# Moving the attention's keys and values beside two projections, and scoring the context in one product

## The chip, the cores and the metric

The kernel runs on one core of a Trainium2 chip. The metric is device time in microseconds (us) of one execution. Before the change the median of three runs was 2660.58 us (2660.32 to 2667.91).

A core has a matrix engine (PE; its weight loads are shown as a row of their own, PEld), a vector engine (DVE), a scalar engine (ACT), a general engine (POOL) and a queue engine for transfers (SP). Each runs its own list of instructions in order and waits on semaphores for the others. Products land in PSUM; DVE and ACT read them from there.

## The reference, cut to what matters

The reference is a transformer block with two mixers, an attention and a gated delta rule, followed by a second block. Only the first block's attention and its neighbours matter here:

```python
aq, ak, av, dq, dk, dv, ... = split_cols(h @ w_in)        # 512 latent tokens
..., cak, cav, ...          = split_cols(hc @ w_in)       # 256 context tokens
q_a  = axial_rope(rms_norm(heads(aq, 8), q_norm_g), row, col)
k_a  = axial_rope(rms_norm(heads(ak, 2), k_norm_g), row, col)
k_ac = rms_norm(heads(cak, 2), k_norm_g)
# per block of 128 queries and per head: at most three blocks of latent keys
# (a band of +-128), all 256 context keys and a sink logit in one softmax
s_loc = where(valid, q @ k_band * 0.125, -1e30);  s_ctx = q @ k_ctx * 0.125
p = softmax(concat([s_loc, s_ctx, s_sink]));      o = p[loc] @ v_band + p[ctx] @ v_ctx
```

There are 8 query heads in two groups that share a key and a value head each, head size 64, and four query blocks: 4 x 2 units of 4 heads, 32 pairs of a head and a query block in all.

## The kernel before, in words

Every large product is made three times with operands split into a rounded and a remainder part (`whi`, `wlo`; `hh`, `hl`), all in the helper `mm3_steps` (L447), which yields after each 8 matmuls. Weights come in blocks of 1 MB through SP's queue (`fetch_w`), are split by ACT (L435) and by DVE or POOL (L108), and two blocks of split weights are held.

In `block1` the projections run one after another. `dense_fm` makes channels on partitions; the short convolution `conv` reads its products out of PSUM on ACT and DVE (L621 to L626), turns them into tokens one tile later (L632) and writes them to DRAM. `dense_tm` makes tokens on partitions; the attention's queries are copied to `aq` by ACT (L658). The order is: keys of the delta rule, its values ("v", two blocks, `dense_fm`), the attention's queries (two blocks, `dense_tm`), and then `rest`: "q" of the convolution and three gates, 72 steps of 8 matmuls.

The attention runs beside the first 28 steps of `rest`. `weave` (through `side_by_side`) takes steps of several generators in turn, in proportion to the numbers that stand beside them:

```python
kv, units = self.window_attention(c, akv, aq, yA)
self.weave((self.take(rest, 28), 28), (self.seq(kv, units), 130))
```

`kv` (19 steps) makes the rotation tables, and for each of six tiles of 128 tokens the norm (`head_rms`: ACT square, DVE sum, POOL power), the rotation (DVE and POOL, L1204 to L1211), the split keys `ks` (ACT L1263, DVE L1264), the split values, and three steps later four transposes (`turn`, L1279) whose result DVE copies into `kT` (L1281). `units` (111 steps) then runs `prep(0)` (the queries of one block: norm, rotation, split `qs`, transposes L1305, copy to `QT` L1307), `front` of the first unit and, for each unit, `back` beside the `front` of the next and the `prep` of the next query block. `front` makes the scores of four heads: two products with the band's keys (L1322, L1323), masks (L1326), four products of 128 columns with the context's keys (L1329), then the row maximum on DVE (L1331), the exponential on ACT (L1335) and, after four heads, the division (L1344). `back` transposes the weights (L1360), splits them (L1363, L1364) and multiplies by the values (L1354).

All of the attention's memory is opened when it starts (`wa1`, `wa2`, and `psS` in PSUM), after the pool of the convolution has been closed. All other PSUM products go through `psum`, which gives four buffers in turn. The context manager is opened with `schedule_with_timeline_sim=True`: the order of the instructions on each engine is laid out when the program is built, from estimated times, and need not be that of the code; on the chip it is fixed.

After the attention the delta rule's first part (`delta`, L904 to L969) runs beside the other 44 steps of `rest`.

Of the kernel before, what the change touches and what calls it, by code (L numbers as in the profile page):

```python
# [78 lines left out]
class Trunk:  # L79
# [438 lines left out]
    def block1(self):  # L518
        nc, I, v = self.nc, self.I, self.v
        b1 = ExitStack()  # L520
# [79 lines left out]
        x_st = [(2 + t, (h[0], h[1], t * P)) for t in range(4)]  # L600
# [6 lines left out]
        evc = ExitStack()  # L607
        kvs = ExitStack()
        evk = self.pool("ev0", 4, side="right", ctx=kvs)
        dgs = ExitStack()  # L610
# [69 lines left out]
        dgs.close()  # L680
        self.dense_fm(0, 2, [cm, xm], conv("v", 8, evk))
        self.dense_tm(0, 2, x_st, keep_aq)

# [15 lines left out]
        with ExitStack() as c:  # L699
            kv, units = self.window_attention(c, akv, aq, yA)  # L700
            self.weave((self.take(rest, 28), 28), (self.seq(kv, units), 130))
            self.flush()
        evc.close()

        yAs = ExitStack()
# [507 lines left out]

    def window_attention(self, ctx, akv, aq, yA):

        nc, I = self.nc, self.I
        one = self.pool("wa1", 1, side="right", ctx=ctx)
        two = self.pool("wa2", 2, side="right", ctx=ctx)
        psc = self.pool("psS", 2, PSUM, ctx=ctx)
        mR = self.T(one, (P, 2, P), "mR", F32R)  # L1220
# [13 lines left out]

        def kv():
            nc.scalar.activation(mR, self.cst[:, C_WP:C_WP + 2 * P].rearrange("p (a b) -> p a b", b=P), AF.Copy)
# [9 lines left out]
            for tt in range(6):  # L1246
                key = tt - 2 if tt >= 2 else tt + 4
                k = akv[:, tt, 0:128].rearrange("p (h f) -> p h f", f=64)
                r = self.head_rms(one, k, 2, "k")
                yield  # L1250
                kn = self.T(one, (P, 2, 64), "kn")
                nc.vector.tensor_tensor(kn, k, r.unsqueeze(2).to_broadcast([P, 2, 64]), ALU.mult)
                if tt >= 2:
                    C, Sn = tabs["k"]
                    kr = self.T(two, (P, 2, 64), "kr")
# [27 lines left out]

        def prep(n):

# [22 lines left out]

        def front(u):
            n, g = u["n"], u["g"]  # L1310
            b0, b1 = max(n - 1, 0), min(n + 1, 3)
            nl = b1 - b0 + 1
            W = nl * P + 256
            u["kb"] = kb = [(b0 + i, i * P) for i in range(nl)] + [(4, nl * P), (5, nl * P + P)]
            Pt = u["Pt"] = self.T(two, (P, 4, 640), "Pt")
            mx = self.T(two, (P, 4), "mx")
            ssum = self.T(two, (P, 4), "ssum")
            for j in range(4):
                h = 4 * g + j
                ps = self.T(psc, (P, 1024), "sc")  # L1320
                lq = QT[n][:, h, :]
                nc.tensor.matmul(ps[:, :nl * P], lq, kT[:, g, 0, b0 * P:(b1 + 1) * P], start=True, stop=False)  # L1322
                nc.tensor.matmul(ps[:, :nl * P], lq, kT[:, g, 1, b0 * P:(b1 + 1) * P], start=False, stop=False)  # L1323
                edge = ([(0, 0)] if n > 0 else []) + ([(1, (nl - 1) * P)] if n < 3 else [])
                for i, (m, o) in enumerate(edge):
                    nc.tensor.matmul(ps[:, o:o + P], self.identR, mR[:, m, :], start=False, stop=i == len(edge) - 1)  # L1326
                for cx, o in kb[nl:]:
                    for w in range(2):
                        nc.tensor.matmul(ps[:, o:o + P], lq, kT[:, g, w, cx * P:(cx + 1) * P],  # L1329
                                         start=w == 0, stop=w == 1)  # L1330
                nc.vector.tensor_reduce(mx[:, j:j + 1], ps[:, :W], AX.X, ALU.max)  # L1331

                nc.vector.tensor_scalar(mx[:, j:j + 1], mx[:, j:j + 1], -0.125, nsink[:, h:h + 1],
                                        ALU.mult, ALU.min)
                nc.scalar.activation(Pt[:, j, :W], ps[:, :W], AF.Exp, bias=mx[:, j:j + 1], scale=0.125,  # L1335
                                     accum_out=ssum[:, j:j + 1])
                yield
# [8 lines left out]

        def back(u):
            n, g, kb, Pt = u["n"], u["g"], u["kb"], u["Pt"]
# [28 lines left out]

        def units():
            us = [dict(n=n, g=g) for n in range(4) for g in range(2)]
            yield from prep(0)  # L1380
            yield from front(us[0])
            for i, u in enumerate(us):
                nxt = us[i + 1] if i + 1 < len(us) else None
                n = u["n"] + 1
                yield from self.side_by_side(
                    (back(u), 11), (front(nxt) if nxt else None, 5), (prep(n) if u["g"] == 0 and n < 4 else None, 6))

        return kv(), units()


# [615 lines left out]
```

## Time and profile before

| | |
|---|---|
| median of three runs | 2660.58 us |
| the profiled execution | 2655.62 us, its span 2653.8 us |
| busy share: PE, DVE, ACT, POOL | 93%, 56%, 38%, 33% |
| mean granted clock of PE | 0.958 of full speed |

The span is what the profiler saw from the first to the last instruction, the profiled execution's own time is 1.8 us more. Starts are counted in us from the span's start. A busy PE is not PE at its peak, since matmuls overlap: the distance between the starts of two neighbours is what one of them costs.

### The profile page before, as it was taken

The numbers are of one execution on the slowest core, as the hardware profiler recorded it, in microseconds if no ns is written. First come the engines' busy times: TensorE is split into PE (matmuls) and PEld (weight loads), VectorE is DVE, ScalarE is ACT, GpSimd is POOL, SyncE is SP. The second block draws the span as 40 slices with busy tenths as digits, with TensorE's granted clock in tenths as the row PEclk, the third lists the DMA queues.
The fourth block names the chain that finished last, engine by engine and source line by source line (L and its number), as shares of the span: only waits on it lengthen the run. The fifth ranks groups of instructions, "written<-read, shape, count | busy, mean of one in ns | idle before, by whom it ended". The sixth has DMA issues, their size and how long they took to land.

```text
span 2653.8 us, 40142 instructions
## 1 busy us (share of the span) xinstructions
PE 2469.4 (93%) x16082; PEld 2097.0 (79%) x16082; DVE 1486.5 (56%) x2532; ACT 1004.2 (38%) x1824; POOL 875.8 (33%) x719
## 2 busy tenths in 40 slices
PE   6897997878999899999998999999998999999998
PEld 3886776556877778799787888888887987888888
DVE  4557658775479942352784887676227357522225
ACT  4545453432442232342663413121224265522332
POOL 2443101000742332455334523232235523523331
PEclk7998998788999999999999999999999999999999
DMA  7231164664535533310012253433212101233331
GB/s 258 74 101 44 56 188 153 219 221 163 179 107 183 167 119 99 100 63 25 9 52 92 94 159 117 126 125 116 64 64 66 44 17 64 85 97 99 96 106 48
DMA packets 249145, 282.53 MB, mean 106 GB/s; under 512 B 12168, under 2 KB 207359, under 8 KB 248703
## 3 DMA queue, kind: packets, MB, share of 16 engines
q1 hardware_dynamic: 225582, 249.86, 29.6%
q10 hardware_dynamic: 23376, 30.11, 3.4%
q8 instruction: 126, 2.06, 0.3%
q14 instruction: 61, 0.49, 0.1%
HBM read 264.06 MB, written 15.88 MB: 105 GB/s over the span
## 4 chain that ended last, share of the span: by engine, by line
PE 70%; DVE 15%; DMA 6%; ACT 4%; issue 3%; POOL 1%; SPq 0%; ACTq 0%; POOLq 0%; DVEq 0%
PE mm L447 60%; DMA wada<-in_w_ada_dram 3%; DVE aacc L242 2%; DVE nt L313 2%; PE sc L1825 2%; PE mm L1850 1%; DVE wlo L108 1%; PE mm L1859 1%; PE mm L1354 1%; DVE tmp L967 1%; ACT whi L435 1%; DVE X L969 1%; DMA ga<-sga 1%; DMA Gb<-grows 1%; PE mm L201 0%
## 5 line engine op out<-in xcount | busy, mean ns | idle before, releaser
L108 POOL TENSOR_TENSOR wlo<-wst,whi 128x1024 fp32r<-128x1024 f32 (+2 forms) x141 | 367.2, 2605 | 769.7 <-ACT whi L435 753.6
L435 ACT ACTIVATE whi<-wst 128x1024 fp32r<-128x1024 f32 (+2 forms) x293 | 287.9, 1031 | 636.4 <-PE mm L447 350.5
L447 PE MATMUL mm<-hmxl,whi 128*128 128x512 f32 (+1 forms) x816 | 314.3, 387 | 4.1 <-DVE hmxl L316 3.2
L447 PE MATMUL mm<-hmxh,whi 128*128 128x512 f32 (+1 forms) x816 | 310.8, 386 | 6.7 <-ACT hmxh L315 6.3
L447 PE MATMUL mm<-hmxh,wlo 128*128 128x512 f32 (+1 forms) x816 | 312.5, 385 | 2.5 <-DVE wlo L108 2.5
L447 PE MATMUL mm<-hidxl,whi 128*128 128x512 f32 (+1 forms) x720 | 280.6, 390 | 7.0 <-DVE hidxl L1478 7.0
L447 PE MATMUL mm<-hidxh,wlo 128*128 128x512 f32 (+1 forms) x720 | 279.9, 389 | 2.4 <-DVE wlo L108 2.4
L447 PE MATMUL mm<-hidxh,whi 128*128 128x512 f32 (+1 forms) x720 | 277.4, 388 | 0.0
L108 DVE TENSOR_TENSOR wlo<-wst,whi 128x1024 fp32r<-128x1024 f32 (+1 forms) x152 | 193.2, 1276 | 148.0 <-ACT whi L435 147.8
L242 DVE SCALAR_TENSOR_TENSOR aacc<-wada,silu,aacc 128x512 f32<-128x512 f32 x280 | 249.0, 937 | 26.0 <-DMA wada<-in_w_ada_dram 25.6
L329 DVE SCALAR_TENSOR_TENSOR xres<-mm,mod,xres 128x512 f32<-128x512 f32 (+1 forms) x122 | 85.0, 703 | 235.9 <-PE mm L447 235.7
L1474 POOL TENSOR_TENSOR nsq<-nt 128x512 f32<-128x512 f32 (+1 forms) x134 | 138.2, 1033 | 149.2 <-ACT nt L1473 127.7
L447 PEld LDWEIGHTS mm<-hmxh,whi 128*128 128x128 f32 x816 | 156.5, 194 | 37.3 <-ACT hmxh L315 7.3
L447 PEld LDWEIGHTS mm<-hmxl,whi 128*128 128x128 f32 x816 | 157.5, 193 | 35.5 <-DVE hmxl L316 4.8
L447 PEld LDWEIGHTS mm<-hmxh,wlo 128*128 128x128 f32 x816 | 157.5, 193 | 33.5 <-DVE wlo L108 3.7
L1478 DVE TENSOR_TENSOR hidxl<-nsq,hidxh 128x512 fp32r<-128x512 f32 (+1 forms) x102 | 75.8, 744 | 172.1 <-POOL nsq L1474 170.6
L447 PEld LDWEIGHTS mm<-hidxl,whi 128*128 128x128 f32 x720 | 136.2, 189 | 37.0 <-DVE hidxl L1478 9.4
L447 PEld LDWEIGHTS mm<-hidxh,wlo 128*128 128x128 f32 x720 | 136.1, 189 | 31.4 <-DVE wlo L108 3.2
L447 PEld LDWEIGHTS mm<-hidxh,whi 128*128 128x128 f32 x720 | 136.0, 189 | 27.8
L1473 ACT ACTIVATE nt<-mm 128x512 f32<-128x512 f32 (+1 forms) x134 | 69.5, 520 | 230.7 <-PE mm L447 224.7
L447 PE MATMUL mm<-whi,h2xh 128*128 128x256 f32 x384 | 110.4, 290 | 3.9 <-ACT raw L1608 2.6
L447 PE MATMUL mm<-wlo,h2xh 128*128 128x256 f32 x384 | 109.2, 287 | 0.0
(517 smaller groups left out, 6033.6 us busy)
## 6 DMA issues: line engine op xcount, KB each, us to landing
wst<-in_w_mlp_dram SPq DMA_DIRECT2D x96, 1024.0 KB, 5.5
wada<-in_w_ada_dram SPq DMA_DIRECT2D x160, 256.0 KB, 2.7
wst<-in_w_in_dram SPq DMA_DIRECT2D x35, 1024.0 KB, 5.4
wada<-in_w_ada_dram SPq DMA_DIRECT2D x48, 512.0 KB, 5.3
wst<-in_w_out_dram SPq DMA_DIRECT2D x10, 1024.0 KB, 7.0
wada<-in_w_ada_dram SPq DMA_DIRECT2D x8, 1024.0 KB, 13.7
xacc<-in_w_out_dram SPq DMA_DIRECT2D x16, 256.0 KB, 2.9
Gb<-grows SPq DMA_DIRECT2D x12, 256.0 KB, 4.2
```

The costliest lines, as they stand in the source:

```text
L108: e.tensor_tensor(out, x, hi.bitcast(F32), ALU.subtract)
L242: nc.vector.scalar_tensor_tensor(acc[j], wt, c, acc[j], ALU.mult, ALU.add)
L313: nc.vector.scalar_tensor_tensor(t, x[:, k, :], a(k), self.rb[n], ALU.mult, ALU.mult)
L329: nc.vector.scalar_tensor_tensor(x[:, m, :], ps[:, :T], gate(m, n), x[:, m, :], ALU.mult, ALU.add)
L435: self.nc.scalar.activation(hi[:, :, c0:c1], st[:, :, c0:c1], AF.Copy)
L447: self.nc.tensor.matmul(ps, lhs[a](k), rhs[b](k), start=first and i == 0, stop=last and i == n - 1)
L967: nc.vector.tensor_tensor(t, Lw[:, j + 1:, j:j + 1].to_broadcast([P, n, w]), x[:, j:j + 1, 0:w].to_broadcast([P, n, w]), ALU.mult)
L969: nc.vector.tensor_tensor(x[:, j + 1:, 0:w], x[:, j + 1:, 0:w], t, ALU.subtract)
L1473: nc.scalar.activation(t, ps[:, :T], AF.Relu)
L1474: nc.gpsimd.tensor_tensor(s2, t, t, ALU.mult)
L1478: self.latest = nc.vector.tensor_tensor(lo, s2, hi.bitcast(F32), ALU.subtract)
L1825: mm = nc.tensor.matmul(ps[:, c0:c1], QT_[:, w, t * P:(t + 1) * P], KT_[:, c0:c1], start=w == 0, stop=w == 1)
```

## The change

Keys and values are no longer made at the head of the attention but beside the convolution's "v" and the query projection, which now are one generator of 48 steps woven with the 19 steps of `kv`. For that `window_attention` is called earlier, with a pool (`wk`) of its own for what lasts (masks, tables, `kT`, the split values) and a pool with two buffers (`wkt`) for the passing tiles of `kv`. `units` opens the rest of the memory when the attention starts, as before. It is woven with 28 steps of `rest` at 28 to 111.

In `front` the band's scores are put at the end of the first PSUM bank of a score tile, so that the context's scores start at column 512, and the context's four products of 128 columns become two of 256.

```diff
+        wks = ExitStack()
+        wk = self.pool("wk", 1, side="right", ctx=wks)
         evk = self.pool("ev0", 4, side="right", ctx=kvs)
...
         dgs.close()
-        self.dense_fm(0, 2, [cm, xm], conv("v", 8, evk))
-        self.dense_tm(0, 2, x_st, keep_aq)
+        keys_, units = self.window_attention(wk, akv, aq)
+        self.weave((self.seq(self.dense_fm_steps(0, 2, [cm, xm], conv("v", 8, evk)),
+                             self.dense_tm_steps(0, 2, x_st, keep_aq)), 48),
+                   (keys_(self.pool("wkt", 2, side="right", ctx=kvs)), 19))
...
         with ExitStack() as c:
-            kv, units = self.window_attention(c, akv, aq, yA)
-            self.weave((self.take(rest, 28), 28), (self.seq(kv, units), 130))
+            self.weave((self.take(rest, 28), 28), (units(c, yA), 111))
             self.flush()
         evc.close()
+        wks.close()
...
-    def window_attention(self, ctx, akv, aq, yA):
+    def window_attention(self, one, akv, aq):
...
-        one = self.pool("wa1", 1, side="right", ctx=ctx)
-        two = self.pool("wa2", 2, side="right", ctx=ctx)
-        psc = self.pool("psS", 2, PSUM, ctx=ctx)
...
-        def kv():
+        def kv(two):
...
-                r = self.head_rms(one, k, 2, "k")
+                r = self.head_rms(two, k, 2, "k")
                 yield
-                kn = self.T(one, (P, 2, 64), "kn")
+                kn = self.T(two, (P, 2, 64), "kn")
...
-        def front(u):
+        def front(u, two, psc):
...
+            s = 512 - nl * P
...
-                nc.tensor.matmul(ps[:, :nl * P], lq, kT[:, g, 0, b0 * P:(b1 + 1) * P], start=True, stop=False)
-                nc.tensor.matmul(ps[:, :nl * P], lq, kT[:, g, 1, b0 * P:(b1 + 1) * P], start=False, stop=False)
+                nc.tensor.matmul(ps[:, s:512], lq, kT[:, g, 0, b0 * P:(b1 + 1) * P], start=True, stop=False)
+                nc.tensor.matmul(ps[:, s:512], lq, kT[:, g, 1, b0 * P:(b1 + 1) * P], start=False, stop=False)
...
-                for cx, o in kb[nl:]:
-                    for w in range(2):
-                        nc.tensor.matmul(ps[:, o:o + P], lq, kT[:, g, w, cx * P:(cx + 1) * P],
-                                         start=w == 0, stop=w == 1)
-                nc.vector.tensor_reduce(mx[:, j:j + 1], ps[:, :W], AX.X, ALU.max)
+                for w in range(2):
+                    nc.tensor.matmul(ps[:, 512:768], lq, kT[:, g, w, 512:768], start=w == 0, stop=w == 1)
+                nc.vector.tensor_reduce(mx[:, j:j + 1], ps[:, s:s + W], AX.X, ALU.max)
...
-        def units():
+        def units(ctx, yA):
+            one = self.pool("wa1", 1, side="right", ctx=ctx)
+            two = self.pool("wa2", 2, side="right", ctx=ctx)
+            psc = self.pool("psS", 2, PSUM, ctx=ctx)
```

## Rows read from the trace of the kernel before

**Rows 1.** Windows: length, busy us of each engine (instructions), granted clock, transfers' share

```profile
core 0: us, PE busy (x) PEld busy (x) DVE busy (x) ACT busy (x) POOL busy (x), PEclk, DMA share, GB/s
110.00:186.00 76.00, 73.64 (x476) 66.27 (x476) 34.98 (x75) 31.84 (x66) 32.61 (x26) 1.00 0.33 101
...
190.50:210.00 19.50, 9.77 (x43) 7.46 (x41) 18.63 (x36) 7.35 (x16) 14.23 (x22) 0.73 0.30 96
210.00:225.00 15.00, 15.00 (x82) 13.39 (x82) 9.71 (x24) 5.94 (x14) 3.25 (x4) 0.78 0.05 16
225.00:362.00 137.00, 124.23 (x700) 97.91 (x699) 89.63 (x192) 74.51 (x151) 24.13 (x20) 0.99 0.22 68
362.00:400.00 38.00, 38.00 (x232) 30.81 (x230) 20.66 (x31) 23.24 (x28) 2.16 (x4) 1.00 0.92 249
400.00:440.00 40.00, 37.08 (x319) 30.37 (x319) 34.70 (x67) 13.07 (x17) 0.90 (x2) 0.91 0.39 121
```

**Rows 2.** Timeline of PE, 200 to 214 us: start, duration, instruction, idle before

```profile
200.59 0.46 PE L1279 MATMUL mm<-identR,ks 128*128 128x128 f32 x4
208.11 0.37 PE L1279 MATMUL mm<-identR,ks 128*128 128x128 f32 x1 [7.06 <-ACT ks L1263]
...
209.90 0.58 PE L1322 MATMUL sc<-kT,QT 128*128 128x256 f32 x1 [0.18 <-ACT QT L1307]
...
213.48 0.63 PE L447 MATMUL mm<-hl,whi 128*128 128x512 f32 x1
213.91 0.63 PE L447 MATMUL mm<-hh,wlo 128*128 128x512 f32 x1
```

**Rows 3.** Waits, 186 to 212 us: who for whom, total us, times, longest

```profile
PE mm L1279 <- ACT ks L1263: 9.4, 2, 7.1
```

**Rows 4.** Groups on DVE, 186 to 212 us: count, busy us, mean ns, idle before

```profile
L1211 DVE TENSOR_TENSOR kr<-kr,ksq 128x128 f32<-128x128 f32 x4 | 4.3, 1076 | 0.0
...
L1281 DVE CAST kT<-mm 128x512 fp32r<-128x512 f32 x5 | 3.4, 681 | 0.2 <-PE mm L1279 0.2
L1264 DVE TENSOR_TENSOR ks<-kr,ks 128x128 fp32r<-128x128 f32 x6 | 2.9, 517 | 0.0
```

**Rows 5.** Timeline of ACT and its queue, 170 to 210 us

```profile
170.33 0.49 ACTq L1229 DMA_DIRECT2D sink<-in_attn_sink_dram  x1
...
177.38 0.63 ACT L1193 ACTIVATE qsq<-aq 128x512 f32<-128x512 f32 x1
...
186.19 0.51 ACT L1263 ACTIVATE ks<-kn 128x128 fp32r<-128x128 f32 x2 [2.55 <-DVE kn L1259]
...
209.27 0.58 ACT L1307 ACTIVATE QT<-mm 128x512 fp32r<-128x512 f32 x1
```

**Rows 6.** Timeline of POOL, 182 to 187 us

```profile
182.01 1.79 POOL L1197 TENSOR_TENSOR qr<-qr,mh 128x8 f32<-128x8 f32 x1
...
184.68 2.22 POOL L1209 TENSOR_TENSOR qsq<-qn,Sq 128x128 f32<-128x128 f32 x4 [0.21 <-DVE qn L1290]
```

**Rows 7.** Timeline of DVE, 212 to 225 us

```profile
212.47 0.69 DVE L1331 TENSOR_REDUCE mx<-sc 128x1 f32<-128x512 f32 x1
...
223.06 1.67 DVE L1344 TENSOR_SCALAR Pt<-Pt,ssum 128x512 f32<-128x512 f32 x4
```

**Rows 8.** Timeline of PE, 222 to 224 us: one head's scores at full clock

```profile
222.31 0.40 PE L447 MATMUL mm<-hh,wlo 128*128 128x512 f32 x1
222.54 0.28 PE L1322 MATMUL sc<-kT,QT 128*128 128x256 f32 x1
222.66 0.28 PE L1323 MATMUL sc<-kT,QT 128*128 128x256 f32 x1
222.78 0.22 PE L1326 MATMUL sc<-mR,identR 128*128 128x128 f32 x1
222.83 0.61 PE L1329 MATMUL sc<-kT,QT 128*128 128x128 f32 x4
223.28 0.33 PE L1322 MATMUL sc<-kT,QT 128*128 128x256 f32 x1
```

**Rows 9.** Waits, 186 to 362 us

```profile
DVE mx L1331 <- PE sc L1329: 13.2, 9, 5.2
```

More of the change, by code (lines that the diff above doesn't have):

```diff
@@ L1254, in kv @@
                     C, Sn = tabs["k"]
-                    kr = self.T(two, (P, 2, 64), "kr")
+                    kr = self.T(two, (P, 2, 64), "krot")
                     self.rope(two, kr, kn, 2, C[:, key], Sn[:, key], 16, "k")
@@ L1282, in turn, with prep @@
                                   ps.rearrange("p (g w t) -> p g w t", g=2, w=2))
-        def prep(n):
+        def prep(n, one, two):
             q = aq[:, n].rearrange("p (h f) -> p h f", f=64)
@@ L1321, in front @@
                 lq = QT[n][:, h, :]
-                nc.tensor.matmul(ps[:, :nl * P], lq, kT[:, g, 0, b0 * P:(b1 + 1) * P], start=True, stop=False)
-                nc.tensor.matmul(ps[:, :nl * P], lq, kT[:, g, 1, b0 * P:(b1 + 1) * P], start=False, stop=False)
+                nc.tensor.matmul(ps[:, s:512], lq, kT[:, g, 0, b0 * P:(b1 + 1) * P], start=True, stop=False)
+                nc.tensor.matmul(ps[:, s:512], lq, kT[:, g, 1, b0 * P:(b1 + 1) * P], start=False, stop=False)
                 edge = ([(0, 0)] if n > 0 else []) + ([(1, (nl - 1) * P)] if n < 3 else [])
                 for i, (m, o) in enumerate(edge):
-                    nc.tensor.matmul(ps[:, o:o + P], self.identR, mR[:, m, :], start=False, stop=i == len(edge) - 1)
-                for cx, o in kb[nl:]:
-                    for w in range(2):
-                        nc.tensor.matmul(ps[:, o:o + P], lq, kT[:, g, w, cx * P:(cx + 1) * P],
-                                         start=w == 0, stop=w == 1)
-                nc.vector.tensor_reduce(mx[:, j:j + 1], ps[:, :W], AX.X, ALU.max)
+                    nc.tensor.matmul(ps[:, s + o:s + o + P], self.identR, mR[:, m, :], start=False,
+                                     stop=i == len(edge) - 1)
+                for w in range(2):
+                    nc.tensor.matmul(ps[:, 512:768], lq, kT[:, g, w, 512:768], start=w == 0, stop=w == 1)
+                nc.vector.tensor_reduce(mx[:, j:j + 1], ps[:, s:s + W], AX.X, ALU.max)
                 nc.vector.tensor_scalar(mx[:, j:j + 1], mx[:, j:j + 1], -0.125, nsink[:, h:h + 1],
                                         ALU.mult, ALU.min)
-                nc.scalar.activation(Pt[:, j, :W], ps[:, :W], AF.Exp, bias=mx[:, j:j + 1], scale=0.125,
+                nc.scalar.activation(Pt[:, j, :W], ps[:, s:s + W], AF.Exp, bias=mx[:, j:j + 1], scale=0.125,
                                      accum_out=ssum[:, j:j + 1])
@@ L1345, in front, with back @@
             yield
-        def back(u):
+        def back(u, two, yA):
             n, g, kb, Pt = u["n"], u["g"], u["kb"], u["Pt"]
@@ L1376, in back @@
             yield
-        def units():
+        def units(ctx, yA):
+            one = self.pool("wa1", 1, side="right", ctx=ctx)
+            two = self.pool("wa2", 2, side="right", ctx=ctx)
+            psc = self.pool("psS", 2, PSUM, ctx=ctx)
             us = [dict(n=n, g=g) for n in range(4) for g in range(2)]
-            yield from prep(0)
-            yield from front(us[0])
+            yield from prep(0, one, two)
+            yield from front(us[0], two, psc)
             for i, u in enumerate(us):
@@ L1385, in units @@
                 yield from self.side_by_side(
-                    (back(u), 11), (front(nxt) if nxt else None, 5), (prep(n) if u["g"] == 0 and n < 4 else None, 6))
-        return kv(), units()
+                    (back(u, two, yA), 11), (front(nxt, two, psc) if nxt else None, 5),
+                    (prep(n, one, two) if u["g"] == 0 and n < 4 else None, 6))
+        return kv, units
     def merge(self, yD, sgd_, xd, ms):
```

## The prediction, as put on record before the result

> **What bounds the kernel now.** I read the page first: PE is busy for 93% of the span and the granted clock is 0.958, so over the whole kernel the matrix engine is the bound, and a change pays only where PE stands still, runs at half clock, or has work taken away. Next I read the windows around the attention [rows 1]. In 110 to 186 us, where the "v" and query projections run, PE is busy 73.6 of 76 us and the other three have slack (DVE 35, ACT 32, POOL 33). In 190.5 to 210 us it is the other way round: PE 9.77 of 19.5, DVE 18.63. Here DVE is the bound, PE starves, and the clock is 0.73, and still 0.78 in the 15 us behind it. From 225 to 362, the eight units of the attention, PE is busy 124 of 137 and DVE 90.
>
> The timeline of PE says what it stood for: 7.06 us in front of a key transpose, whose operand ACT had not finished [rows 2]; all such waits sum to 9.4 us [rows 3]. Behind that transpose stand, in PE's fixed order, the query transposes, the first scores at 209.90 and then the next projection tile. The groups on DVE in that stretch name the culprit: the three largest of the keys' groups alone take 10.6 us [rows 4].
>
> So keys and values are late, not the queries: the first query block is ready for its norm at 177.38, yet its transposed copy ends at 209.85 [rows 5]. The small loads that `kv` needs are issued at 170.33, so in this kernel it could not start earlier.
>
> **The change part by part.**
>
> *1. The stall in front of the first scores goes.* It is worth the idle time, 19.5 - 9.77 = 9.7 us [rows 1], and what the half clock behind it costs. The clock has two levels, so a mean of 0.78 over 15 us is 0.44 of it, 6.6 us, at 1.2 GHz, which does 3.3 us of full-clock work: 3.3 lost. One 512-column matmul costs 213.91 - 213.48 = 0.43 us there [rows 2] against 222.54 - 222.31 = 0.23 at full clock [rows 8]. In 190.5 to 210 the mean of 0.73 is 10.5 us at half clock, nearly as long as the idle time; I put 1 us on it. Together 14 us are to be had; nothing is the other end.
>
> What is late next? `prep(0)` is a chain of its own: from 177.38, square 0.63, sum about 0.7, power 1.79, norm about 0.7, rotation 2.22, then add, rounding, remainder and one copy at 0.6 to 0.7 each [rows 5, 6]. That is about 9 us, and 11 to 12 with hand-overs: about 189. `front` of the first unit then needs four maxima at 0.69, the exponential of the last head and 1.67 for the division [rows 7], about 9 us: 198. In that time PE has the first tile pair of `rest`: 48 matmuls at 0.23 are 11 us from 186.5, up to 197.5, plus 2.5 us of scores. So PE is nearly covered up to the first `back`; I leave 2 us standing. Gain 12 us. If the cover fails because the first scores come ahead of those 48 matmuls in PE's list, PE waits for `QT` as it now waits for keys, and most of this term is gone (a rival below).
>
> *2. The context's products.* Four of 128 columns cost 223.28 - 222.83 = 0.45 us, one of 256 costs 0.12 [rows 8]; 0.45 - 0.24 = 0.21 us a head, and 32 heads give 6.7 us. The other end is nothing: the mask's product in the same rows, also of 128 columns, costs only 222.83 - 222.78 = 0.05, and four at that price would be 0.2, no more than the two that replace them. I take 0.18, near the row of the four themselves, since the first of the pair may now wait for its weights behind the short mask product: 5.8 us of PE's work. How much is on the path? From 225 to 362 neither PE nor DVE is full [rows 1], but DVE waits 13.2 us for just these products before a maximum [rows 9]; so I count two thirds, 4 us. The maximum and the exponential keep their widths; that they now cross a bank border costs nothing that a row here could show, and I put 0.
>
> On this the Trainium skill's "TensorE: Matmul & The Clock Gate", section "Back-to-back issue gap", speaks against the change: it prices an isolated matmul at 134 cycles for 128 columns and 262 for 256, so four short ones and two long ones would cost the same within 12 cycles, and the 32 heads would give 0.2 us by estimate. The trace does not agree, with 0.45 against 0.24 us. The same section has a second figure, about 81 ns for each short product in a stream with weight loads; by it the estimate is 0.11 us a head, 3.4 us in all.
>
> *3. The moved work beside "v" and queries.* The 24 key transposes go with it. They cost PE the same in either place, some 0.07 us each, 1.7 us in all: added here, taken away there, zero. DVE gets about 20 us, ACT about 7 and POOL about 9 (powers and rotations, which stand ahead of the convolution's products and the weights' remainders on POOL). DVE then has 55 of 76 us, and it still fits. The four small loads move up on ACT's queue, past "v"'s evictions, at up to 0.49 us for each issue [rows 5]; SP's queue is passed by none. What the move adds is waits in lists that have no slack behind them: `ks` on ACT waits for DVE, 2.55 us where seen [rows 5], and behind it on ACT now stand the convolution's reads of PSUM and the copies to `aq`, for which PE waits once its four buffers are full. One tile lasts 24 x 0.23 = 5.5 us for latent tokens, about half for context and for queries, so one such wait is hidden by one or two tiles in hand; two in a row are not. Ends: 0, and 6 tiles x 2.5 = 15 us if none is hidden. The window has 2.4 us of idle PE now. I take 2 us of new stalls. The transposes themselves come three steps of `kv` behind their operands, seven to eight steps of PE, and should not wait.
>
> *4. Behind the attention.* The delta rule's first part follows. In 362 to 400 PE is full, transfers are at 0.92, and from 400 to 440 DVE is busy 34.7 of 40 [rows 1]. Its vector work begins when the attention's ends, and PE's tiles of `rest` are the same in number, so I let the gain through whole; if not, it is the fourth case.
>
> *Sum:* -12 - 4 + 2 = -14 us. Against the profiled execution, 2655.6 us (its span of 2653.8 and 1.8 around it), that is 2641.6. The median of the runs shown, 2660.6, stands 5 us above that execution; new runs will be of the same kind, so I forecast 2660.6 - 14 = 2646.6 us.
>
> **The rivals.**
> - *Forecast, 0.64:* 2646.6 us. Its own range: term 1 from 8 to 14, term 2 from 2 to 7, term 3 from 0 to 5, so about 2639 to 2652.
> - *Short products are as cheap as the mask's, 0.08:* the context's part saves nothing, -12 + 2 = -10, 2650.6 us. For it: the mask's 0.05 us; against it: the row of the four. This is what the first rule of the page named above gives.
> - *The stall moves to the queries, 0.12:* PE's list has `QT`'s transposes and the first scores before enough projection tiles. For it: the list of now does just this with the keys, because estimated times ran ahead of real ones. Of the 9.7 us only those that the keys added beyond the queries' chain go, about 3, and of term 2 stay 4; with 2 us of stalls, -5: 2655.6 us.
> - *Given back in the delta rule, 0.07:* its broadcasts (transfers at 0.92) stand on SP between weight loads that PE's progress paces, so that its start doesn't move, and only PE's lesser work stays: about -3, 2657.6 us.
> - *Slower, 0.09:* the keys' chain stops the convolution. Six tiles, each with two waits of ACT or DVE of about 2.5 us, stand ahead of evictions, PE runs out of its four PSUM buffers in a stage where it was full, and the clock falls with it. It decides once more than 16 us are lost, over half of those 6 x 2 x 2.5 = 30; with 26 lost it is +10: 2671 us. For it: strict order on ACT and DVE, and no idle time of PE to absorb it. Against it: DVE and ACT are under half busy there, and `kv` now has two buffers for its tiles.
>
> **How the numbers follow.** A measurement of this kernel tells about 0.3%, 8 us, from no change. Faster by more than that are the first two cases, 0.72; within it the third and fourth, 0.19; slower 0.09. For the range: its lower end takes the whole of terms 1 and 2 with no stall, -21, from the profiled execution's level (2655.6), 2635; its upper end takes in the third and fourth case and a loss that just cancels the gain, 2661.
>
> **What would show it.** Right: no wait of PE for `ks` of more than 1 us and first scores at about 190 instead of 209.90; the clock at 1.00 from 190 to 225; 64 instead of 128 context products, at 0.12 us each; the units' last PE work some 14 us earlier, and the delta rule's first matmul as much. The window of the "v" and query projections should be longer by no more than 4 us, of which 1.7 are the transposes. Wrong: a wait for `QT` of several us before the first scores (third case); PE idle for over 8 us between 110 and 190, with waits of evictions behind `ks` (slower); or an earlier attention and an unchanged end of the delta rule's first part (fourth).

## The result, and the profile after

The change made the kernel slower. The changed kernel takes 2675.84 us (median of 20 runs, 2664.47 to 2683.51) beside 2660.39 for the kernel before (20 runs); the ratio is 1.0051 with a 95% interval of 1.0042 to 1.0061 (the two medians alone give 1.0058). The forecast was 2646.6 with a range up to 2661. The profiled execution took 2671.32 us, its span is 2669.5, 15.7 more than before. (Line numbers after are 2 to 7 higher.)

First the windows that answer to [rows 1]:

```profile
core 0: us, PE busy (x) PEld busy (x) DVE busy (x) ACT busy (x) POOL busy (x), PEclk, DMA share, GB/s
110.00:186.00 76.00, 67.99 (x393) 59.91 (x394) 42.75 (x98) 33.74 (x69) 36.98 (x44) 0.91 0.30 93
190.50:210.00 19.50, 19.50 (x133) 17.85 (x133) 13.95 (x18) 6.93 (x13) 12.15 (x11) 1.00 0.33 104
210.00:225.00 15.00, 5.72 (x30) 4.72 (x28) 13.87 (x20) 10.78 (x15) 10.22 (x10) 0.76 0.24 75
225.00:362.00 137.00, 121.96 (x638) 95.22 (x639) 86.95 (x192) 72.52 (x152) 20.54 (x14) 0.94 0.19 58
```

PE is full in 190.5 to 210, where it had stood half the time. But it lost 5.6 us in 110 to 186, a window that begins with the last "k" tiles in both kernels, and in 210 to 225 it is busy for 5.7 of 15. The timeline of PE shows what stands there, to be laid beside [rows 2] and [rows 8]:

```profile
210.34 0.28 PE L1326 MATMUL sc<-kT,QT 128*128 128x256 f32 x1
...
210.64 0.45 PE L1333 MATMUL sc<-kT,QT 128*128 128x256 f32 x2
210.93 0.28 PE L1326 MATMUL sc<-kT,QT 128*128 128x256 f32 x1
...
217.80 0.53 PE L1326 MATMUL sc<-kT,QT 128*128 128x256 f32 x1 [4.53 <-ACT Pt L1338]
...
225.35 0.58 PE L1326 MATMUL sc<-kT,QT 128*128 128x256 f32 x1 [5.09 <-ACT Pt L1338]
```

The first scores come at 210.34, as late as before (209.90). The wait for `ks` of [rows 3] is gone, and PE now waits for the exponentials that must free the two score buffers. From the last query eviction to the last write of the attention's output these waits are:

```profile
PE sc L1326 <- ACT Pt L1338: 13.3, 8, 5.1
PE mm L1357 <- ACT ph L1366: 3.9, 5, 1.1
PE mm L1363 <- ACT gate L665: 2.4, 2, 1.7
PE mm L1363 <- DVE ct L647: 2.3, 1, 2.3
```

The other loss lies far ahead of the attention. The timeline of ACT and its queue, 70 to 79 us:

```profile
70.36 0.33 ACTq L1231 DMA_DIRECT2D sink<-in_attn_sink_dram  x1
70.80 0.38 ACTq L1232 DMA_DIRECT2D rope<-in_rope_dram  x1
...
72.41 0.34 ACTq L784 DMA_DIRECT2D dtb<-in_dt_bias_dram  x1
...
78.85 0.45 ACTq L786 DMA_DIRECT2D cstd<-in_cst_dram  x1
```

and that of DVE:

```profile
73.30 3.36 DVE L108 TENSOR_TENSOR wlo<-wst,whi 128x1024 fp32r<-128x1024 f32 x1
76.58 1.48 DVE L1242 TENSOR_TENSOR Cq<-rope,gq 128x256 f32<-128x256 f32 x1
...
79.80 0.87 DVE L624 SCALAR_TENSOR_TENSOR cy<-mm,vec,cy 128x255 f32<-128x255 f32 x2
```

The code traces the keys' loads behind the delta gates and beside "v". The planner issued them at 70.36, 100 us earlier than in [rows 5]. I read this as the early pool's doing, which gives them free memory; it was not tested by itself. The gates' loads, the tables' arithmetic and the first convolution stand behind them. The keys' chain itself starts behind the last "k" tile. Its norms run while the first three "v" tiles are made, its transposes beside the rest of "v" and the queries (the views of the tiles `kr` and `ks`: norms, their first use and transposes, first and last start):

```profile
L1199 DVE TENSOR_REDUCE kr<-ksq x6: 271/276/280, 136.8 to 151.8; 128x2 f32<-128x128 f32 x6
L1254 DVE TENSOR_TENSOR kn<-akv,kr x6: 283/558/1372, 138.8 to 153.7; 128x128 f32<-128x128 f32 x6
L1281 PE MATMUL mm<-identR,ks x24: 222/244/305, 156.0 to 200.1; 128*128 128x128 f32 x24
```

How much was lost by when is seen where ACT reads the last "k" tile and the third "v" tile out of PSUM, first before, then after:

```profile
124.23 0.68 ACT L621 ACTIVATE cy<-mm,vec 128x512 f32<-128x512 f32 x1
...
135.62 0.69 ACT L621 ACTIVATE cy<-mm,vec 128x512 f32<-128x512 f32 x1 [2.29 <-PE mm L447]
```

```profile
135.19 0.69 ACT L623 ACTIVATE cy<-mm,vec 128x512 f32<-128x512 f32 x1
...
150.39 0.69 ACT L623 ACTIVATE cy<-mm,vec 128x512 f32<-128x512 f32 x1 [1.40 <-PE mm L447]
```

By the last "k" tile, ahead of every step of the chain, 11.0 us are lost; while the norms run, 3.8 more.

Up to the first "v" tokens PE's waits are these (before: 2.1 for `cy`, 1.4 for `ct`, 1.4 for `csg`, 0.7 for `hl`):

```profile
PE mm L447 <- POOL hl L321: 4.4, 2, 3.6
PE mm L825 <- issue: 3.8, 1, 3.8
PE mm L634 <- POOL csg L628: 2.0, 1, 2.0
PE mm L447 <- DVE cy L625: 1.9, 1, 1.9
```

The waits are not all of it. The windows from 60 us to the first "v" tokens and from 110 to 120 us, before and after:

```profile
60.00:136.60 76.60, 69.29 (x425) 62.42 (x426) 41.84 (x77) 39.91 (x70) 36.15 (x27) 0.96 0.26 82
110.00:120.00 10.00, 10.00 (x47) 8.14 (x47) 4.65 (x11) 3.98 (x9) 4.23 (x4) 1.00 0.22 66
```

```profile
60.00:151.40 91.40, 75.75 (x425) 67.46 (x426) 55.13 (x119) 45.28 (x88) 42.24 (x41) 0.87 0.24 72
110.00:120.00 10.00, 5.99 (x24) 5.36 (x25) 7.01 (x18) 5.40 (x10) 3.88 (x4) 0.60 0.38 124
```

Of the 14.8 us, 8.3 are more idle time of PE and 6.5 the same 425 products taking longer, at a mean granted clock of 0.87 instead of 0.96. In 110 to 120 us, around the wait of 3.8 us at L825, it is 0.60.

I cut each profiled span at five places that all kernels have: first "v" tokens leaving, last query projection evicted, last write of the attention's output (`yAl`), the delta rule's first state (`S`), first use of `xres` behind it. Lengths in us:

| | to "v" | "v" and queries | attention | to first state | delta rule | rest | span |
|---|---|---|---|---|---|---|---|
| before | 136.6 | 50.0 | 175.1 | 134.4 | 161.4 | 1996.3 | 2653.8 |
| after | 151.4 | 49.7 | 171.3 | 138.7 | 165.7 | 1992.7 | 2669.5 |
| difference | +14.8 | -0.3 | -3.8 | +4.3 | +4.3 | -3.6 | +15.7 |

The delta rule's windows, before and after:

```profile
496.10:657.50 161.40, 134.79 (x2446) 99.49 (x2446) 111.33 (x244) 56.56 (x104) 5.92 (x5) 0.88 0.63 203
```

```profile
511.10:676.80 165.70, 139.68 (x2446) 104.27 (x2446) 111.34 (x244) 55.88 (x104) 5.91 (x5) 0.85 0.61 195
```

What the delta rule takes more, 4.3 us, is not idle time (26.6 and 26.0 us) but the same 2446 products at a lower mean clock.

### The profile page after: what moved, and what is told of

It reads as the page before. It is cut to its first block, busy times and chain, and to the rows that moved or that the text cites. A ratio compares the mean times of both kernels' runs of the same rounds, so it can differ in the third digit from the quotient of the medians.

```text
span 2669.5 us, 40036 instructions
## 1 busy us (share of the span) xinstructions
PE 2475.0 (93%) x16018; PEld 2100.3 (79%) x16018; DVE 1488.6 (56%) x2532; ACT 1007.9 (38%) x1827; POOL 873.6 (33%) x719
## 4 chain that ended last, share of the span: by engine, by line
PE 70%; DVE 14%; DMA 6%; ACT 5%; issue 3%; POOL 2%; SPq 0%; ACTq 0%; POOLq 0%; DVEq 0%
PE mm L447 60%; DMA wada<-in_w_ada_dram 3%; DVE aacc L242 2%; DVE nt L313 2%; PE sc L1832 1%; PE mm L1857 1%; DVE wlo L108 1%; PE mm L1357 1%; PE mm L1866 1%; DVE X L973 1%; DVE tmp L971 1%; PE u L1076 1%; DMA Gb<-grows 0%; ACT whi L435 0%; DMA wst<-in_w_in_dram 0%
## 5 line engine op out<-in xcount | busy, mean ns | idle before, releaser
L1481 POOL TENSOR_TENSOR nsq<-nt 128x512 f32<-128x512 f32 (+1 forms) x134 | 138.5, 1035 | 147.0 <-ACT nt L1480 124.4
L447 PE MATMUL mm<-hh,whi 128*128 128x512 f32 x256 | 103.9, 406 | 5.9 <-ACT gate L665 2.1
## 6 DMA issues: line engine op xcount, KB each, us to landing
wada<-in_w_ada_dram SPq DMA_DIRECT2D x8, 1024.0 KB, 14.2
```

The lines of the kernel that those rows point to most:

```text
L447: self.nc.tensor.matmul(ps, lhs[a](k), rhs[b](k), start=first and i == 0, stop=last and i == n - 1)
L1481: nc.gpsimd.tensor_tensor(s2, t, t, ALU.mult)
```

## The experiments

Times are medians of 5 to 12 runs (20 for before and after); ratios are to runs of the kernel before on the same chip, with 95% intervals. Those runs had medians of 2659.7 to 2663.6 us, so a difference between two rows is sure to no better than some 4 us.

| kernel | first "v" tokens | attention | last write | median | ratio |
|---|---|---|---|---|---|
| before | 136.6 | 175.1 | 361.7 | 2660.4 | 1 |
| after | 151.4 | 171.3 | 372.4 | 2675.8 | 1.0051 (1.0042 to 1.0061) |
| e1_context | 137.5 | 177.7 | 365.2 | 2654.5 | 0.9970 (0.9958 to 0.9981) |
| e2_move_only | 151.3 | 175.8 | 376.7 | 2675.7 | 1.0053 (1.0036 to 1.0070) |
| e3_keys_held | 152.8 | 169.6 | 371.8 | 2671.1 | 1.0036 (1.0024 to 1.0047) |
| e5_space_only | 144.2 | 177.2 | 371.3 | 2658.8 | 0.9988 (0.9976 to 1.0000) |
| e6_keys_behind_v | 148.3 | 169.4 | 367.7 | 2666.1 | 1.0013 (0.9998 to 1.0028) |
| e7_gate_first | 151.8 | 162.7 | 364.2 | 2656.0 | 0.9978 (0.9968 to 0.9987) |
| e8_both | 147.8 | 163.1 | 360.9 | 2660.2 | 0.9994 (0.9984 to 1.0004) |
| e9_gates_left | 147.3 | 166.0 | 367.4 | 2672.6 | 1.0033 (1.0019 to 1.0046) |
| e10_delay_15 | 149.0 | 167.5 | 366.5 | 2659.3 | 0.9996 (0.9986 to 1.0006) |
| e11_delay_7 | 142.0 | 167.8 | 359.8 | 2655.8 | 0.9989 (0.9979 to 0.9999) |
| e12_no_chain | 146.6 | 170.3 | 364.9 | 2662.8 | 1.0009 (1.0000 to 1.0019) |
| e13_no_max | 151.8 | 163.0 | 364.5 | 2664.4 | 1.0015 (1.0005 to 1.0024) |
| e14_before24 | 138.3 | 179.2 | 367.4 | 2662.4 | 1.0001 (0.9992 to 1.0010) |
| e15_after24 | 151.5 | 155.6 | 356.8 | 2661.6 | 1.0002 (0.9992 to 1.0011) |
| e16_context24 | 137.4 | 174.9 | 362.3 | 2657.4 | 0.9989 (0.9980 to 0.9998) |
| e17_context20 | 137.4 | 160.3 | 347.7 | 2647.8 | 0.9950 (0.9937 to 0.9962) |
| e18_context20_delay | 149.9 | 166.5 | 366.4 | 2668.5 | 1.0025 (1.0014 to 1.0036) |
| e19_held24 | 146.4 | 160.1 | 360.6 | 2664.4 | 1.0006 (0.9994 to 1.0018) |

**The two halves of the change.** e1 adds only the context product to the kernel before, e2 takes only it out of the changed one.

```
-                for cx, o in kb[nl:]:
-                    for w in range(2): ... 128 columns each
+                for w in range(2):
+                    nc.tensor.matmul(ps[:, 512:768], lq, kT[:, g, w, 512:768], start=w == 0, stop=w == 1)
```

> The kernel before with the 256-column context product alone; keys, values, pools and queues stay where they were. Theory A (the slowdown comes from the keys' early work getting ahead of the delta gates): this part is innocent, 64 fewer products in a stretch that PE bounds, so 1 to 7 us faster than before (forecast of this step: 4), and the stall for ks ahead of the first scores is still there at about 9 us. Rival (the score tile's new offset or the wider product itself costs, through PSUM banks or the exponentials): equal to before or slower by up to 5 us.

> The changed kernel with the four short context products put back; the keys and values are still made beside the projections. Theory A: the whole slowdown is in the move, so this is 14 to 21 us slower than before, that is 1 to 7 us slower than the changed kernel. Rival (the context product is what slows): equal to before or faster, about 2645 to 2660 us.

Both came out as the first theory had it: the product alone is 6 us faster than before, with 9.3 us of waits for `ks` still there, and the move alone is 15.2 us slower. The slowdown is the move's.

**Where ahead of "v" it is lost.** e3 orders the keys' loads and chain behind the gates' last transfer; e5 puts an unused pool of the keys' size into the kernel before.

```
+        with self.tc.issue_after(self.gates_end.ins):        # e3: also around every step of keys_
             keys_, units = self.window_attention(wk, akv, aq)
```

```
+        dead = self.T(self.pool("dead", 1, side="right", ctx=kvs), (P, 6544), "dead")   # e5
         evk = self.pool("ev0", 4, side="right", ctx=kvs)
```

> The changed kernel, but the keys' and values' four loads and every step of their chain are ordered on ScalarE's queue behind the delta gates' last DMA; the memory map stays that of the changed kernel. Theory A (early keys' work ahead of the gates on ScalarE and VectorE costs the 14.8 us before the first 'v' tile): the first 'v' eviction comes back from 150.4 to 136 to 140 us, and the kernel is 10 to 16 us faster than the changed one, so 0 to 4 us on either side of before. Rival L (memory map: the keys' pool pushes the gates' and the convolution's buffers onto memory that comes free later, and this delays the gates' loads): the first 'v' eviction stays at 148 us or later and the time stays within 4 us of the changed kernel. Rival C (on record: the keys' chain stops the convolution in the 'v' stage): PE idles over 8 us between 140 and 190 us, and the time is again over 8 us slower than before.

> The kernel before with an unused pool of the keys' size (26 KB in each partition) opened below the convolution's and the gates' buffers and closed with them; nothing else is moved. It isolates the memory map: same buffers, other places, with the same order of the gates' loads on ScalarE as in e3_keys_held. Theory A: within 3 us of before, first 'v' eviction at 135.6 to 138 us. Rival L: 10 to 15 us slower than before, first 'v' eviction at 146 us or later, with the gates' loads at 78 us or later. If both causes share: 4 to 8 us slower.

Neither theory held. Held keys gave back 4.7 us, and "v" came no earlier: once released, the chain ran into the first "v" tiles (norms from 139.4 to 154.0 us, the last "k" tile read at 133.0; PE busy 13.3 of 20 us in 130 to 150). Space alone delays "v" by 7.6 us, all of it by the last "k" tile (131.8), with these waits, and costs nothing at the end:

```profile
PE mm L447 <- POOL hl L321: 2.7, 1, 2.7
PE mm L634 <- POOL csg L628: 2.2, 2, 1.4
PE mm L823 <- issue: 2.1, 1, 2.1
```

e6 puts the chain behind a "v" tile, on ACT and DVE. I had meant the third, but its condition takes the first (read at 136.4, the chain's first square at 137.1); so does e8's. In e9 and e19 the condition asks for latent tokens as well, and there it is the third (e19: 144.7 and 145.6). e9 also lays the gates' buffers on memory that is free from the start; e12 leaves out the keys' norm, rotation, split and transposes.

```
+                if which == "v" and self.v_first is None:    # e6, in conv; e9, e19: and name == "x"
+                    self.v_first = ya_, yd_
+                with self.tc.issue_after(a_.ins), self.tc.issue_after(d_.ins):  # round each step of keys_
```

```
+        dg = self.pool("dg", ctx=hcs)                                        # e9, instead of side="right"
```

```
+            for g in range(2):                                               # e12, instead of the chain
+                for w in range(2):
+                    nc.scalar.activation(kT[:, g, w, :]..., akv[:, :, 0:P], AF.Copy)
```

> The changed kernel, but every step of the keys' chain is ordered behind the convolution of the third 'v' tile, on ScalarE's and on VectorE's queue, so that it runs only where no 'k' tile is left; the four loads stand behind the gates' last DMA; the memory map is the changed kernel's. Theory C' (the keys' VectorE and ScalarE steps, put between the steps of the 'k' tiles and their norms wherever the planner finds room, stop PE there: 7 to 8 us beyond the 7.6 us that the space alone costs by the first 'v' tokens): the first 'v' tokens leave at 144 to 146 us as in e5_space_only (151.4 in the changed kernel), the last query projection is evicted at 194 to 197 us (201.1), and the kernel is 6 to 12 us faster than the changed one. Rival D (VectorE's work costs the same wherever it stands in the projections): the chain stops the 'v' stage instead, last query projection at 199 us or later, time within 4 us of the changed kernel.

> As e6_keys_behind_v, and the delta gates' buffers lie on the other side of the memory, in space that nothing used before them, so their loads need not wait for the norm's buffers. If the lost 7.6 us by the first 'v' tokens come from the gates' loads landing late, those tokens leave at 136 to 139 us; if from the convolution's own buffers being on memory that comes free late, still at 143 us or later. Time against e6_keys_behind_v: 0 to 7 us faster by the first, the same within 3 us by the second. e5_space_only lost 7.6 us there and was no slower at the end, so a gain there need not reach the end either.

> The changed kernel without the keys' chain: norm, rotation, split and transposes of the keys are left out, four ScalarE copies put other numbers in the keys' place; loads, tables, values, queries, units and memory map stay. What is left of the loss ahead of 'v' is the space, the loads and the tables. Theory C' (the chain's steps between the steps of the 'k' tiles cost 4 to 8 us): first 'v' tokens at 144 to 147 us instead of 151.4, and the kernel 5 to 10 us faster than the changed one. Rival (the loads and tables ahead of the gates are the cause): tokens at 149 us or later, time within 3 us of the changed kernel. From the last query projection to the last kTd 253 to 256 us in either case if the keys were no bound of that stretch.

e6 is 9.7 us faster than the changed kernel, as the theory had it, but "v" came at 148.3 and the last query eviction at 198.3, outside both forecasts. Behind the third tile "v" comes earlier (e19: 146.4), and the chain costs in the next stage: 54.1 us from "v" to the last query eviction in e9 and e19, 50.0 in e6. In e9 the gates' loads are issued at 1.2 to 5.1 us, and "v" still leaves at 147.3, no earlier than in e19: the loads are not what is late in the space's part; which other buffer is was not tried. Its time is 6.5 us above e6, but with the chain held at another tile this doesn't price the gates' buffers. e12 gives the price of the chain ahead of "v": 151.4 - 146.6 = 4.8 us, most of it in the first three "v" tiles (the last "k" tile is read at 134.2, against 135.2). So, if the parts add, the 14.8 us are 7.6 of space (e5), 4.8 of chain, and 2.4 left for loads, tables and values. Against my expectation e12 stretched the way from the last query eviction to the last `kTd` (transposed keys of the delta rule) from 255 to 261 us, and gained 13 us.

**The stall that came back.** ACT in the changed kernel, 215 to 225 us:

```profile
215.67 1.28 ACT L1338 ACT_TABLE_LOAD   x1
216.97 0.69 ACT L1338 ACTIVATE Pt<-sc,mx 128x512 f32<-128x512 f32 x1
...
221.06 1.28 ACT L627 ACT_TABLE_LOAD   x1 [2.65 <-issue]
...
223.22 1.28 ACT L1338 ACT_TABLE_LOAD   x1 [0.23 <-DVE mx L1336]
224.51 0.69 ACT L1338 ACTIVATE Pt<-sc,mx 128x512 f32<-128x512 f32 x1
```

A sigmoid of the "q" convolution stands between two exponentials, and each change of table costs 1.28 us. The Trainium skill's "ScalarE: Activation LUTs", section "Table sets: the hidden batching unit", asks to batch calls by table set; its example puts a load at about 2.7 us, and the rows have 1.28. The second exponential also waited for its maximum, which stands on DVE behind the queries' norm and the convolution:

```profile
217.49 2.85 DVE L1292 TENSOR_TENSOR qn<-aq,qr 128x512 f32<-128x512 f32 x1 [0.87 <-POOL qr L1201]
220.26 0.74 DVE L625 SCALAR_TENSOR_TENSOR cy<-mm,vec,cy 128x511 f32<-128x511 f32 x1
...
221.75 1.27 DVE L1334 TENSOR_REDUCE mx<-sc 128x1 f32<-128x512 f32 x2
```

e7 exchanges the convolution with a gate, e8 joins this with e6, and e13 leaves out the scores' maxima.

```
-            yield from self.dense_fm_steps(0, 2, [xm], conv("q", 0, ev))     # e7: moved behind szd
             yield from self.dense_fm_steps(0, 2, [xm], gate(szd))
+            yield from self.dense_fm_steps(0, 2, [xm], conv("q", 0, ev))
```

```
-                nc.vector.tensor_reduce(mx[:, j:j + 1], ps[:, s:s + W], AX.X, ALU.max)   # e13
+                nc.vector.tensor_copy(mx[:, j:j + 1], nsink[:, h:h + 1])                 # exp: scale=0.001
```

> The changed kernel with the 'q' convolution and the first gate (szd) exchanged in the work that runs beside the attention, so that only the gate's evictions, and no convolution, sigmoid or table change, stand on ScalarE and VectorE while the first units' scores wait for their exponentials. Theory S (the stall left the keys and came back at the exponentials, because VectorE's and ScalarE's queues hold the 'q' convolution ahead of the maxima): PE's wait for the exponentials falls from 13.3 us to 6 us or less, the last half of the output is written 5 to 10 us earlier than 372.4 us, and the kernel is 0 to 10 us faster than the changed one. Rival (two score buffers alone set that wait): it stays above 10 us and the time within 3 us of the changed kernel.

> Both edits: keys behind the third 'v' tile, and the first gate ahead of the 'q' convolution. By the two theories together the gains add: 8 to 20 us faster than the changed kernel, so 2656 to 2668 us down to 2650 us or less if the gate's part is large. By the rivals: within 4 us of the changed kernel.

> The changed kernel without the maxima of the scores: the exponential takes the sink alone as its bias and a small scale, so that it waits for the scores and not for VectorE. Theory S (the stall came back at the exponentials because VectorE's queue holds the maxima behind the queries' norm and the convolution): PE's wait for the exponentials falls from 13.3 us to 6 us or less, and the last half of the output is written 5 us or more before 372.4 us. Rival (ScalarE itself is late there: weight halves, table changes): the wait stays above 9 us. Whether the time follows depends on the delta rule's front: if the stretch from the last query projection to the last kTd stays at 255 us, the time stays within 4 us of the changed kernel.

In e13 the wait for the exponentials falls to

```profile
PE sc L1326 <- ACT Pt L1335: 6.7, 4, 3.1
```

so about half of it goes with DVE's maxima. (The planner also put 16 fewer products ahead of the last write there, 744 instead of 760.) In e7 the wait did not fall, it rose:

```profile
PE sc L1326 <- ACT Pt L1338: 16.2, 10, 4.4
```

and yet the last write came 8.2 us earlier and the kernel was 19.9 us faster than the changed one. The size of PE's wait was not what decided. Nor did e7 test the rule on table sets: the sigmoid's first table load in the attention came at 265.5 us instead of 221.1, but there are nine table loads in that stage, and seven in the changed kernel. What e7 also has is 35 fewer products ahead of the last write (725). e8 gained 15.6 us, less than e7 alone: its last write came 3.3 us earlier than e7's, but its delta rule took 176.6 us at a mean clock of 0.82, and e7's 160.8 at 0.89.

**Is a delay carried?** e10 and e11 put 66 and 33 products of 512 columns into the kernel before, ahead of "v".

```
+        with self.tc.issue_after(self.gates_pe.ins):
+            for i in range(66):
+                nc.tensor.matmul(ps, h[0][:, 0, 0:P], h[0][:, 0, :], start=i == 0, stop=i == 65)
```

> The kernel before with 66 extra 512-column products on TensorE behind the delta gates, about 15 us of PE work ahead of the 'v' projections and nothing else: it asks whether the 14.8 us that the change loses ahead of the first 'v' tokens are enough for its slowdown. Theory P (everything behind hangs on PE's chain, so a delay there is carried to the end): 10 to 18 us slower than before (2671 to 2679 us), first 'v' tokens at 150 to 152 us, and 255 us from the last query projection to the delta rule's last kTd as in all kernels so far. Rival Q (delays there are taken up later, by transfers that are late anyway, so the change's slowdown has another source): under 5 us slower.

> The same with 33 products, about 7.5 us. Theory P: half as much, 4 to 10 us slower than before. Rival Q, which e5_space_only's 7.6 us without a loss speaks for: within 3 us of before. If 15 us cost 15 and 7.5 cost nothing, the delta rule decides, by how its steps meet the transfers and the clock, and not by adding up.

Nothing of it is seen at the end: in e10 "v" is 12.4 us late, in e11 5.4, and the times are the same as before or 0.1% less. But e10 is no clean test: its attention had become 7.6 us shorter, though its code is the same. The windows from the last query eviction to the last write say how, before and in e10:

```profile
186.60:361.70 175.10, 152.60 (x840) 121.67 (x839) 121.58 (x256) 91.29 (x188) 44.98 (x51) 0.94 0.21 65
```

```profile
199.00:366.50 167.50, 144.38 (x801) 114.20 (x800) 121.88 (x257) 90.88 (x187) 45.77 (x51) 0.94 0.23 67
```

39 fewer products stand ahead of the last write: the planner, whose estimated times had moved, listed fewer steps of the gates' projections there. Hence the next question, how many of the 72 steps of `rest` stand beside the units. e14 to e17 take 24 or 20 instead of 28, in the kernel before, the changed one and e1; e18 is e17 with e10's delay, e19 is e6 with 24 and the chain behind the third "v" tile.

```
-            self.weave((self.take(rest, 28), 28), (units(c, yA), 111))
+            self.weave((self.take(rest, 24), 24), (units(c, yA), 111))       # and (rest, 48) in delta
```

> The kernel before with 24 instead of 28 of the 72 steps of the 'q' and gate projections beside the attention, the other four behind it, beside the delta rule's start. Theory U (the delta rule's start hangs on the attention's last write, 131 to 141 us behind it): four steps are 32 products of 0.227 us, so the last write comes 4 to 8 us earlier and the kernel is 3 to 8 us faster than before. Rival W (TensorE's whole work up to the last gate sets the start): the last write comes earlier, the time stays within 3 us.

> The changed kernel with the same edit. Theory U: last write at 364 to 369 us instead of 372.4, 3 to 8 us faster than the changed kernel, so 2668 to 2673 us. Rival W: within 3 us of the changed kernel.

> The kernel before with the 256-column context product and 24 steps. Theory U: its 4 to 6 us and the 3 to 8 us of the steps add: 2646 to 2653 us, faster than both kernels. Rival W: 2652 to 2657 us, as e1_context.

> The same with 20 steps. Theory U: another 2 to 7 us off e16_context24 while TensorE has work enough to fill the attention; less once the units' own chain (maxima, exponentials, transposes) is what is left, and a loss if the gates' last step becomes late for the delta rule. Rival W: no gain, or up to 4 us slower than e16_context24, since TensorE idles more in the attention.

> e17_context20 (2647.8 us) with the 66 products of e10_delay_15 ahead of 'v'. If delays there are carried: first 'v' tokens about 12 us later, attention from the last query projection to its last write still 158 to 163 us, and 8 to 15 us slower than e17_context20 (2656 to 2663 us). If a later stage takes them up: attention again 160 us and time within 4 us of e17_context20. If the attention's length changes again by over 4 us, TensorE's list is what decides, and the delay is not measured by itself.

> The changed kernel with the keys' chain behind the third 'v' tile (9.7 us faster than the changed kernel by itself) and 24 steps of the gates beside the attention (14.2 us by itself). If the two parts of the loss add: 2648 to 2656 us. If both act on the same wait: 2658 to 2664 us, no better than 24 steps alone.

The same windows, after, e15 and e17:

```profile
201.10:372.40 171.30, 146.98 (x760) 115.59 (x759) 109.05 (x223) 89.23 (x177) 37.45 (x30) 0.93 0.19 61
```

```profile
201.20:356.80 155.60, 133.32 (x696) 105.65 (x695) 108.60 (x222) 89.75 (x175) 36.67 (x29) 0.91 0.19 56
```

```profile
187.40:347.70 160.30, 126.36 (x665) 98.65 (x664) 115.58 (x253) 87.94 (x182) 44.38 (x50) 0.87 0.18 52
```

In e15 64 products fewer stand ahead of the last write, it comes 15.6 us earlier, and 14.2 us of them reach the end. e17 idles PE for 34 us in the attention against 22.5 before, and is the fastest of all, faster than both kernels. But e14, also with 64 products fewer, has an attention 4.1 us longer: the "q" tokens leave at 250 to 317 us instead of 238 to 281, and the mean clock is 0.86 instead of 0.94. e16 gained nothing over e1; and in e18 the attention grew by 6.2 us, the last write came 18.7 us later, and 20.7 us were lost, so the delay is not measured by itself there either. e19 is no better than 24 steps alone; as it holds the chain elsewhere than e6, whether e6's gain adds is open.

## Why the prediction was wrong, step by step

- **Step 1 (the stall, -12): the cover failed, and nothing of the 12 us came.** The wait for `ks` went as forecast, and first scores came 9.2 us behind the last query eviction instead of 23.3. Then "what is late next" was the exponential, for which I had counted only the last head's: 13.3 us of waits for it (0.5 before) took the place of 9.4. PE's idle time in the attention went from 175.1 - 152.6 = 22.5 to 171.3 - 147.0 = 24.3 us. The move alone (e2) leaves the attention at 175.8 us, 175.1 before. This is close to my third case, in which the stall moves on, but that case named `QT`, and what was late was the exponential. e13 puts about half of it on DVE's maxima.
- **Step 2 (context products, -4): right.** A pair takes 0.29 us up to the next product (210.64 to 210.93), where four took 0.45: 0.16 us a head, 5 us in all. My 0.24 for a pair had the price of a band product, 0.12, twice; the 0.18 that I took is near. With the move in both, PE's busy time in the attention is 151.7 without the product (e2) and 147.0 with it, 4.7 us; e1 is 6 us faster than before. The 0.2 us that the Trainium skill's "TensorE: Matmul & The Clock Gate", section "Back-to-back issue gap", gives by its first figure is not what these runs show.
- **Step 3 (moved work, +2): the step that failed most.** It measured +14.8 us. I had priced the waits of the chain alone, beside "v" and the queries. From the first "v" tokens on the move cost nothing there, 49.7 us against 50.0 (48.0 without the chain, e12, which bears out the 1.7 us of transposes). Up to those tokens the chain cost 4.8 us (e12), most of it in the first three "v" tiles and within my 0 to 5. But 11.0 us were lost by the last "k" tile, ahead of every step of the chain: 7.6 come with an unused pool alone (e5), which is no work at all but new addresses for the other buffers, and e12, with loads, tables and values but no chain, has lost 10.0 there. What I took from the diff as a place in time is only a place in the code; the planner starts work as soon as its operands and its memory are free, and the diff moved `wk`'s memory to before the gates. The space's term was not in my sum nor in a rival.
- **Step 4 (all carried): unsettled.** The last write came 10.7 us later, and the end 15.4 (medians). In single experiments 9.6 us of a later write cost -1.6 (e5), 18.7 cost 20.7 (e18), and 15.6 earlier gave 14.2 (e15). Over the 20 kernels of the table a line through last write and median has slope 0.86, correlation 0.74 and a scatter of 5 us; through the delta rule's first state, which came 15.0 us later in the changed kernel, it has 1.00, 0.82 and 4.3. These places are signs of the time, not shown causes. Behind them the clock counts: the delta rule, whose own code no edit touched, took 158 to 177 us in the 20 profiles, the longer the lower its mean clock (correlation -0.88; 0.90 in the shortest, 0.82 in the longest). The 20 runs of the changed kernel lie 19 us apart, and their times go with the mean clock too (-0.80). Why the clock differs from edit to edit was not tried.
- **The rivals.** The slower one (2671) had the price, and by luck: its mechanism, the keys' chain stopping the convolution in the "v" stage, is there, but with 4.8 us and not 26. Short products as cheap as the mask's is refuted by e1. That the delta rule takes the gain back was not tested alone.
- **The signs I named.** Right: no wait for `ks`, the clock at 1.00 from 190.5 to 210, 64 context products, the stage from the first "v" tokens to the last query eviction no longer. On the edge: PE idle for 8.0 us between 110 and 190, where over 8 was to speak for the slower case. Wrong: a pair of context products in 0.29 us and not 0.24, first scores at 210 and not 190, 0.76 for the clock in 210 to 225, the units' end later and not earlier.

## What to carry to other kernels

Where a planner orders the queues, opening a pool earlier is a change of schedule: ask first when the new memory is free and whose addresses move, then what will start then and in front of whom. When a stall goes, follow the next operation on every engine's own list, not on the one that stalled. And a full PE is not the aim by itself: the fastest kernel here (e17, 0.9950 of before) has 34 us of idle PE in the attention and fewer products in front of its last write. That is no rule either, since 24 steps gave nothing over e1 (e16).

## What the runs showed that I had not expected

Edits that take no work away and add none move this kernel by as much as the change itself: 28 or 24 steps in the changed kernel 14.2 us, the order of two projections 19.9 us, an unused pool 7.6 us at "v" and nothing at the end. A difference of 5 us between two versions of one edit says little here about the edit's own cost. And a delay need not be idle time: 6.5 of the 14.8 us ahead of "v" and the delta rule's 4.3 are unchanged products at a lower granted clock.
